# One-hot rows of the dense expert gates from bit products on TensorE

## The chip, the cores and the metric

The kernel runs on one core of a Trainium2 chip. The metric is device time in microseconds (us), from the first to the last instruction of one launch, as the median of several runs. The engines are named as in the profile: PE is TensorE (PEld its weight loads), DVE is VectorE, ACT is ScalarE, POOL is GpSimd, SP is SyncE, which issues most DMAs.

## The reference, cut to what matters

The program is a two-layer backbone over 512 latent and 256 context tokens of width 1024: a mixer and a PEER expert layer in each layer. The change lies in the expert layer alone:

```
def block(xt):                                       # 128 tokens
    s = scores of the token against 2 x 128 keys, for 8 heads
    sv, si = lax.top_k(s, 16)                        # per head and key set
    cand = sv[:, :, 0, :, None] + sv[:, :, 1, None, :]
    cs, ci = lax.top_k(cand, 16)                     # 16 experts (i, j) a head
    gate = softmax(cs)
    a = einsum('nd,nhkd->nhk', xt, u[eidx])
    w = gate * gelu(a)
    return einsum('nhk,nhkd->nd', w, v[eidx])
```

A token selects 8 x 16 = 128 experts out of 128 x 128, each named by two indices i and j below 128.

## The kernel before, in words

For 384 of the latent tokens (ND, three blocks of 128) the expert layer is computed densely: all 16384 experts, with a gate that is zero where an expert was not selected. The other tokens take their experts by gathered rows (`gather`, DMAs issued by POOL, sums on DVE).

`peer` (L1330 on) runs once a layer, in two stages. The routing stage has the pools `ps` (PSUM: tag `pj` with 2 buffers of one bank, `big` with 2 of two banks, `po` with 2 of one bank) and `wts`. `route` makes the scores (`scores`, top 16 by `top16` on DVE) and then, block by block and half by half, `select`, which leaves the indices fi, fj and the gate g as [128 tokens, 128 selections]. Its scratch comes from `alloc`, 5 buffers of [128, 1024] shared with the lists of the top 16. Once both halves of a dense block are selected, `gate_build` (L1044) makes its dense gates. In the same stage `dense_u` (L1105) computes the first product for 18 experts columns (layer 0) or 27 (layer 1) ahead, from weights that SP loads (L182) and that ACT and DVE or POOL split in two (L185, L188). The dense stage follows: 128 steps of first and second products (L1112, L1161), which multiply by the gates read back from DRAM (`load_gates`, L1139, L1151).

`gate_build` transposes fi, fj and g with TensorE (L1055), so that selections lie on the partitions and tokens in the free dimension, and splits each index in its upper and lower bits (L1056 to L1059). Then it goes through eight chunks of 16 tokens. For a chunk DVE compares the bits with a ramp (L1070, `up` and `low`, four instructions), POOL multiplies the low rows of j by the gate (L1073), and eight products of an upper and a lower row (L1084, `ghot`, [128, 4 tokens, 128]) give the one-hot rows of i and of j for four tokens each. DVE makes five of the eight, POOL three (`GENG`). For every token a matmul of the two rows (L1090, `gps`, 128x128, fp32) sums the 128 selections into the token's gates [i, j]. Eight tokens fill a `big` tile, which ACT copies to `G` [i, j, 16 tokens] (L1092), written with a step of 16 elements. One DMA a chunk, issued by ACT, puts G into DRAM (L1093). A layer has 24 chunks, 96 groups of four tokens ("pairs" of one-hot rows), 768 gate matmuls and 48 copies.

The order on each engine is set by the Tile scheduler, by program order as priority and by when it reckons an instruction to be ready; engines then run their queues in order. `issue_after` and `later` hold parts back. All waits are its own.

Of the kernel before, what the change touches and what calls it, by code (L numbers as in the profile page):

```python
# [22 lines left out]
ND = 384        # latent tokens whose experts are computed densely  # L23
# candidate segments of the 16x16 sums: rows a0..a1 keep their first nb columns
SEGS = [(0, 1, 16), (1, 2, 8), (2, 4, 5), (4, 8, 3), (8, 16, 1)]
NCAND = sum((b - a) * n for a, b, n in SEGS)
GENG = "vpvpvvvp"           # engines that make the one-hot rows in turn: Vector, Pool
UPRE = 18, 27               # by layer: experts (., j) whose first product runs ahead of the second
EARLY = 350                 # gathered rows of layer 0 that go ahead of its dense part
LATE = 64                   # of layer 0's, those that are left to the mixer of layer 1  # L30
# [30 lines left out]
def _cst_layout():  # L61
    off = 0
    for name, n in (("ident", 128), ("ones", 128), ("perm", 128), ("mf", 128), ("mb", 128),
                    ("iota", 128), ("start", 16), ("cos", 512), ("sin", 512)):
        CST[name] = (off, n)
        off += n
    return off
# [5 lines left out]
def constants():  # L73
# [27 lines left out]
    put("start", np.array(starts)[None, :])  # L101
    return c


class Kern:
    def __init__(self, ctx, tc, a, dbg=None):
# [8 lines left out]
        self.wcnt, self.wlo, self.ghot = 0, WL1, 0  # L115
# [12 lines left out]
        self.yd = self.dr.tile([2, D, 768], F32, name="yd")  # L128

# [10 lines left out]
    @contextmanager  # L140
    def mixing(self):
        """pools of the parts between the expert layers"""
        tc = self.tc
        with tc.tile_pool(name="wts", bufs=2, reuse_waits="tile") as self.pw, \
                tc.tile_pool(name="ps", bufs=1, space=bass.MemoryType.PSUM, reuse_waits="tile") as self.ps:
            yield
# [9 lines left out]
    def later(self, offset=1 << 20):  # L156
        """what is issued inside gives way to what is issued up to `offset` later"""
# [20 lines left out]
    def weight(self, src, shape):  # L178
        """src: DRAM AP of `shape` ([128, k, n], 1024 elements a row); returns (hi, lo)."""
# [28 lines left out]
    def projN(self, ps, w2, x, b):  # L208
        """ps [128 tok of block b, 256] = x^T w, w2 = the two halves of k."""
# [10 lines left out]
    def mod_prep(self):  # L220
# [9 lines left out]
        # column 1 adds up the partitions  # L230
# [4 lines left out]
    def mod(self, l, parts):  # L235
        """rows m_parts of layer l (streams ctx, lat) to DRAM; parts 1 and 4 as (1 + m) g."""
# [79 lines left out]
    def mod_rows(self, l, parts):  # L316
        """mod for the latents alone with the products on Vector, a step for 128 rows of the weights."""
# [18 lines left out]
    def mod_out(self, l, m, q, ps):  # L336
        """a quarter of part m from its product: bias, gain, to DRAM."""
# [20 lines left out]
    def rstd(self, ss, n, shape, scale=None):  # L358
        """(ss / n + eps) ** -0.5"""
# [16 lines left out]
    def xpose(self, x, xt, b):  # L376
        """x [128 tok, 1024] into xt = (hi, lo) [128, 8, T] at block b."""
# [11 lines left out]
    def norm1(self, l, s, src, nb, rows=None):  # L389
        """modulated norm of the blocks src[b]; returns their transposed halves."""  # L390
# [20 lines left out]
    def even_prep(self):  # L411
# [21 lines left out]
        # mLSTM gate rows: forward heads on partitions 0-3, backward heads on 32-35  # L433
# [10 lines left out]
    def gates(self, s, xt, nb, bb):  # L444
        """gate rows, stabilisers and the columns drawn from them, for blocks bb..bb+nb."""
# [33 lines left out]
        # columns  # L479
# [13 lines left out]
        # chunk totals on every partition  # L493
# [3 lines left out]
        # off-diagonal column biases QG[:, target, direction, source, head]  # L497
# [18 lines left out]
    def sigmoid(self, x, out, n):  # L516
        """out = exp(min(x, 0) - ln(1 + exp(-|x|))), n columns"""
# [8 lines left out]
    def ml_pair(self, s, xt, nb, bb, pr, P):  # L526
        """mLSTM heads 2 pr, 2 pr + 1 of blocks bb..bb+nb: projections; returns the rest,
        which writes the outputs transposed to DRAM."""
# [4 lines left out]
        # conv + silu of q (two padded copies) and k  # L533
# [22 lines left out]
        # v with a column of ones, output gate  # L556
# [28 lines left out]
        def front(hh, b):  # L585
# [21 lines left out]
            plan = []   # (direction, first slot, first source, count) off the diagonal  # L607
# [56 lines left out]
    def pipe(self, units, front, back):  # L664
        """front of a unit is issued ahead of the back of the one before it"""
# [856 lines left out]
```

## Time and profile before

| | |
|---|---|
| time of the runs, median of 3 | 4348.12 us (4344.39 to 4353.43) |
| span of the profiled execution | 4350.6 us |
| busy: PE, PEld | 3739.3, 3297.7 us |
| busy: DVE, ACT, POOL | 3715.8, 1603.3, 2683.4 us |
| DMA | 1093 MB, mean 251 GB/s |
| gate matmuls, L1090 | 1536, 231.8 us |
| one-hot products, L1084 | 240 on DVE, 144 on POOL |
| copies of the gates, L1092 | 96, 184.0 us |

Busy time is the time in which an engine had an instruction in work, and PE and PEld overlap. A mean over the whole span hides that the stages have different limits, so the stages are read one by one. The two gate stages are the short stretches from 1304 to 1514 us (layer 0) and from 3172 to 3385 us (layer 1). A line of the timeline merges neighbours of one kind, so that its length can hold short idle times; what stands in square brackets is the idle time ahead of it and what ended that.

### The profile page before, as it was taken

How to read it: one execution, taken by the hardware profiler on the slowest of the kernel's cores; microseconds unless marked ns; L12 is line 12 of the kernel's file. 1: busy time of each engine (PE TensorE's matmuls, PEld its weight loads, DVE VectorE, ACT ScalarE, POOL GpSimd, SP SyncE). 2: the span in 40 equal slices, each digit the busy share in tenths (PEclk: the TensorE clock that was granted, in tenths of full speed). 3: DMA queues.
4: the chain of work that ended last, by engine and by line, in shares of the span. 5: the costliest groups of instructions: out<-in, count | busy, mean ns of one | idle time of the engine just before them, and what ended most of it. 6: DMA issues, size and time to landing. Idle time of an engine off the chain costs nothing.

```text
span 4350.6 us, 58785 instructions
## 1 busy us (share of the span) xinstructions
PE 3739.3 (86%) x20576; PEld 3297.7 (76%) x20576; DVE 3715.8 (85%) x6089; ACT 1603.3 (37%) x2676; POOL 2683.4 (62%) x1886
## 2 busy tenths in 40 slices
PE   7977666756687699999999968899886999999999
PEld 5776654445567689988889857787875899999987
DVE  6479989979999998898989989747999887777788
ACT  4433433412115533333333325443245433333333
POOL 3146777656656677777878667112577676666664
PEclk9998888878798999999999989999989999999999
DMA  5554888788742499999899988423234987887878
GB/s 192 187 185 158 276 284 280 263 308 317 241 135 109 184 337 336 332 320 327 318 331 335 341 301 290 160 84 125 94 126 168 321 309 272 285 287 269 288 264 313
DMA packets 382487, 1093.10 MB, mean 251 GB/s; under 512 B 32671, under 2 KB 134375, under 8 KB 376046
## 3 DMA queue, kind: packets, MB, share of 16 engines
q0 software_dynamic: 147456, 536.94, 34.8%
q1 hardware_dynamic: 224942, 491.58, 32.9%
q10 hardware_dynamic: 9792, 60.82, 3.4%
q8 instruction: 162, 2.65, 0.2%
q14 instruction: 135, 1.11, 0.1%
HBM read 1020.96 MB, written 68.26 MB: 250 GB/s over the span
## 4 chain that ended last, share of the span: by engine, by line
PE 40%; DVE 25%; issue 15%; DMA 11%; POOL 7%; ACT 2%; SPq 0%; POOLq 0%; DVEq 0%; ACTq 0%
PE dacc L1161 17%; PE dA L1112 14%; POOL uv L998 4%; DVE ghot L1084 4%; DMA uv<-in_pr_u_dram,ix 3%; DMA draw<-in_uT_dram 3%; DVE junkv L1011 3%; DMA uv<-in_pr_v_dram,ix 2%; PE ops L214 1%; DVE wlo L188 1%; DVE pacc L1024 1%; PE pqps L204 1%; DVE sel L916 1%; DVE gup L1070 1%; DVE sel L913 1%
## 5 line engine op out<-in xcount | busy, mean ns | idle before, releaser
L1161 PE MATMUL dacc<-dhi,dw 128*128 128x512 f32 x3072 | 989.1, 392 | 3.4 <-ACT dw L1154 1.8
L998 POOL DMA_INDIRECT uv<-in_pr_v_dram,ix x512 | 685.6, 1339 | 405.0 <-DVE pacc L1024 297.6
L998 POOL DMA_INDIRECT uv<-in_pr_u_dram,ix x512 | 685.2, 1338 | 373.6 <-DVE pa L1011 204.3
L1011 DVE CUSTOM_DVE_ANT_0 junkv<-uv,x 128x1024 bf16<-128x1024 f32 x512 | 734.7, 1435 | 39.5 <-DMA uv<-in_pr_u_dram,ix 35.5
L1024 DVE SCALAR_TENSOR_TENSOR pacc<-uv,pw,pacc 128x1024 f32<-128x1024 f32 x508 | 705.1, 1388 | 26.9 <-DMA uv<-in_pr_v_dram,ix 23.0
L1161 PEld LDWEIGHTS dacc<-dhi,dw 128*128 128x128 f32 x3072 | 579.9, 189 | 120.7 <-ACT dw L1154 2.1
L1101 ACT CAST dhi<-draw 128x1024 fp32r<-128x1024 f32 x467 | 489.2, 1050 | 463.6 <-DMA draw<-in_uT_dram 165.9
L1161 PE MATMUL dacc<-dlo,dw 128*128 128x512 f32 x1536 | 604.4, 394 | 11.1 <-DVE dlo L1102 11.0
L1102 POOL TENSOR_TENSOR dlo<-draw,dhi 128x1024 fp32r<-128x1024 f32 x210 | 545.5, 2598 | 95.6 <-ACT dhi L1101 91.9
L188 POOL TENSOR_TENSOR wlo<-wraw,whi 128x1024 fp32r<-128x1024 f32 x111 | 280.0, 2523 | 426.0 <-ACT whi L185 282.1
L1151 DVE TENSOR_TENSOR dz<-dz,dG 128x384 f32<-128x384 f32 x256 | 402.4, 1585 | 89.9 <-ACT dz L1121 88.5
L1154 ACT CAST dw<-dz 128x384 fp32r<-128x384 f32 x256 | 131.4, 513 | 690.8 <-PE dacc L1161 669.8
L1102 DVE TENSOR_TENSOR dlo<-draw,dhi 128x1024 fp32r<-128x1024 f32 x257 | 336.1, 1308 | 27.3 <-ACT dhi L1101 18.1
L185 ACT CAST whi<-wraw 128x1024 fp32r<-128x1024 f32 x195 | 204.3, 1049 | 416.6 <-PE pqps L204 101.5
L1112 PE MATMUL dA<-xth,dhi 128*128 128x384 f32 x1688 | 334.8, 340 | 10.1 <-ACT dhi L1101 6.9
L1161 PEld LDWEIGHTS dacc<-dlo,dw 128*128 128x128 f32 x1536 | 289.8, 189 | 70.1 <-DVE dlo L1102 13.3
L1112 PE MATMUL dA<-xtl,dhi 128*128 128x384 f32 x1688 | 327.4, 335 | 0.0
L1112 PEld LDWEIGHTS dA<-xth,dhi 128*128 128x128 f32 x1688 | 305.1, 189 | 28.5 <-ACT dhi L1101 7.8
L1112 PE MATMUL dA<-xth,dlo 128*128 128x384 f32 x1688 | 326.7, 334 | 0.0
L1090 PE MATMUL gps<-ghot 128*128 128x128 f32 x1536 | 231.8, 307 | 104.5 <-DVE ghot L1084 80.2
L1090 PEld LDWEIGHTS gps<-ghot 128*128 128x128 f32 x1536 | 211.2, 216 | 126.3 <-issue 84.4
L1112 PEld LDWEIGHTS dA<-xtl,dhi 128*128 128x128 f32 x1688 | 296.7, 188 | 0.0
(379 smaller groups left out, 6836.6 us busy)
## 6 DMA issues: line engine op xcount, KB each, us to landing
draw<-in_pr_v_dram SPq DMA_DIRECT2D x256, 512.0 KB
draw<-in_uT_dram SPq DMA_DIRECT2D x211, 512.0 KB
wraw<-in_wb_dram SPq DMA_DIRECT2D x150, 512.0 KB
gd<-gch ACTq DMA_DIRECT2D x48, 1024.0 KB
dG<-gd SPq DMA_DIRECT2D x30, 1536.0 KB
wraw<-in_mod_t_dram SPq DMA_DIRECT2D x48, 512.0 KB
wraw<-in_uT_dram SPq DMA_DIRECT2D x45, 512.0 KB
wraw<-in_mod_w_dram SPq DMA_DIRECT2D x32, 512.0 KB
```

What stands on the lines that cost most here:

```text
L185: nc.scalar.copy(hi, raw)
L188: eng.tensor_tensor(lo, raw, hi.bitcast(F32), op=OP.subtract)
L998: nc.gpsimd.indirect_dma_start(out=t, out_offset=None, in_=a[table], in_offset=bass.IndirectOffsetOnAxis(ap=ix[:, c:c + 1], axis=0))
L1011: nc.vector.tensor_tensor_reduce(out=junk, in0=u, in1=x, op0=OP.mult, op1=OP.add, scale=1.0, scalar=0.0, accum_out=A[:, c:c + 1])
L1024: nc.vector.scalar_tensor_tensor(acc, v, W[:, c:c + 1], acc, op0=OP.mult, op1=OP.add)
L1084: eng.tensor_tensor(h.rearrange("p t (a b) -> p t a b", b=16), up[:, e, t0:t0 + 4, :].unsqueeze(3).broadcast_to([128, 4, 8, 16]), low[:, e ...
L1090: nc.tensor.matmul(ps[:, t0 - 8 * q + t, :], hot[0][:, t, :], hot[1][:, t, :], start=True, stop=True)
L1101: nc.scalar.copy(hi, raw)
L1102: eng.tensor_tensor(lo, raw, hi.bitcast(F32), op=OP.subtract)
L1112: nc.tensor.matmul(A, u[ui][:, k, :], xt[xi][:, k, 0:ND], start=(i == 0), stop=(i == 23))
L1151: nc.vector.tensor_tensor(z3, z3, self.G[:, :, j % JG, :], op=OP.mult)
L1161: self.nc.tensor.matmul(acc[b][:, h, :], w[wi][:, 128 * b:128 * b + 128], v[vi][:, 512 * h:512 * h + 512], start=(j == 0 and i == 0), stop ...
```

## The change

The one-hot rows are no longer products of an upper and a lower row on DVE and POOL. Each index is split in seven bits, on DVE, in the layout that it has (tokens on the partitions). Bit e is kept as 2^e or 0, beside a plane of ones, as bf16. The planes of a block are written to DRAM (`bd`, 512 KB) and read back four chunks at a time (256 KB) with (token, bit) on the partitions. There a matmul with constant coefficients (`gB`, block diagonal over the 16 tokens of a chunk) gives, for a token and each value n, 1 minus the number of bits that differ from those of n: 1 where the index is n, 0 or less elsewhere. One matmul of 512 columns makes four tokens. ACT takes the positive part of those of i (Relu), DVE that of j times the gate (`scalar_tensor_tensor`). The gate matmuls stay. The copy of the products walks with indices outside and 8 tokens inside, so that its writes are runs of 8 elements and its reads of PSUM step by 128 elements.

New constants are `coef` (128 columns) and `tmask` (16 columns) in `cst`. `gate_build` gets `alloc` and takes three of the shared buffers a block. `fi` and `fj` become halves of one tile. Comments and docstrings are gone.

```
-GENG = "vpvpvvvp"           # engines that make the one-hot rows in turn: Vector, Pool
...
+    bits = (p[None, :] >> np.arange(7)[:, None]) & 1
+    coef = np.concatenate([(2.0 * bits - 1.0) / 2.0 ** np.arange(7)[:, None], 1.0 - bits.sum(0)[None, :]], 0)
+    put("coef", np.tile(coef, (16, 1)))
+    put("tmask", p[:, None] // 8 == np.arange(16)[None, :])
...
+        self.bd = self.dr.tile([ND // 128, 1024, 256], BF16, name="bd")
...
+    def gate_consts(self):
+        nc = self.nc
+        self.gB = self.wk.tile([128, 16, 128], BF16, name="gB")
+        nc.vector.tensor_tensor(self.gB, self.c("coef")[:, None, :].broadcast_to([128, 16, 128]),
+                                self.c("tmask").unsqueeze(2).broadcast_to([128, 16, 128]), op=OP.mult)
+
+    def gate_build(self, b, sel, alloc):
         nc, wk = self.nc, self.wk
...
+        _, g, fij, _ = sel
+        pl = alloc().bitcast(BF16).rearrange("p (e x) -> p e x", e=8)
+        nc.gpsimd.memset(pl[:, 7, :], 1.0)
+        for s in range(2):
+            bu = alloc().bitcast(U32).rearrange("p (e x) -> p e x", e=8)
+            nc.vector.tensor_copy(bu[:, 7, :], fij[:, 128 * s:128 * s + 128])
+            for e in range(7):
+                nc.vector.tensor_scalar(bu[:, e, :], bu[:, 7, :], 1 << e, None, op0=OP.bitwise_and)
+            nc.vector.tensor_copy(pl[:, 0:7, 128 * s:128 * s + 128], bu[:, 0:7, :])
+        nc.sync.dma_start(self.bd[b].rearrange("(t e) x -> t e x", e=8), pl)
+        pt = self.po([128, 128], "gtp")
+        nc.tensor.transpose(pt, g, self.ident)
+        gT = wk.tile([128, 128], F32, name="gT", tag="gT", bufs=2)
+        nc.scalar.copy(gT, pt)
         for c in range(8):
...
+            if c % 4 == 0:
+                bits = wk.tile([128, 4, 256], BF16, name="gbits", tag="gbits", bufs=2)
+                nc.sync.dma_start(bits, self.bd[b].rearrange("(c p) x -> p c x", p=128)[:, c:c + 4, :])
             G = wk.tile([128, 128, 16], F32, name="gch", tag="gch", bufs=2)
             for q in range(2):
                 ps = self.big([128, 8, 128], "gps")
                 for t0 in (8 * q, 8 * q + 4):
                     hot = []
+                    for s in range(2):
+                        d = self.po([128, 4, 128], "gds")
+                        nc.tensor.matmul(d, bits[:, c % 4, 128 * s:128 * s + 128], self.gB[:, t0:t0 + 4, :],
+                                         start=True, stop=True)
                         h = wk.tile([128, 4, 128], F32, name="ghot", tag="ghot", bufs=6)
...
+                        if s == 0:
+                            nc.scalar.activation(h, d, AF.Relu)
+                        else:
+                            t = 16 * c + t0
+                            nc.vector.scalar_tensor_tensor(
+                                h, d, 0.0, gT[:, t:t + 4].unsqueeze(2).broadcast_to([128, 4, 128]),
+                                op0=OP.max, op1=OP.mult)
                         hot.append(h)
                     for t in range(4):
                         nc.tensor.matmul(ps[:, t0 - 8 * q + t, :], hot[0][:, t, :], hot[1][:, t, :],
                                          start=True, stop=True)
-                nc.scalar.copy(G[:, :, 8 * q:8 * q + 8].rearrange("p j t -> p t j"), ps)
+                nc.scalar.copy(G[:, :, 8 * q:8 * q + 8], ps.rearrange("p t j -> p j t"))
             nc.scalar.dma_start(self.gd[8 * b + c], G)
```

## Rows read from the trace of the kernel before

**Rows 1.** Stretches: length; busy PE, PEld, DVE, ACT, POOL; granted clock, DMA share, GB/s.
```profile
1304.00:1514.00 210.00, 151.03 (x964) 140.31 (x962) 198.46 (x293) 111.09 (x86) 141.48 (x109) 0.90 0.37 143
...
3450.00:4200.00 750.00, 750.00 (x3792) 682.76 (x3791) 591.53 (x579) 274.11 (x364) 504.90 (x284) 1.00 0.82 285
...
3172.00:3385.00 213.00, 157.48 (x988) 145.51 (x987) 201.98 (x304) 115.61 (x97) 148.34 (x116) 0.91 0.40 153
```
**Rows 2.** Chain that ended last, 1290 to 1530 us, by line; two pieces in layer 1.
```profile
by line: DVE ghot L1084 32.0%; issue 18.0%; DVE gup L1070 10.6%; DVE glow L1070 8.0%; POOL glow L1073 3.4%; DVE wlo L188 3.2%; DMA draw<-in_uT_dram 3.1%; DVE sel L965 2.7%; POOL ghot L1084 2.5%; DVE sel L969 2.3%; POOL dlo L1102 2.2%; DVE s
...
3384.67 3.88 DMA gd<-gch
3388.62 3.98 DMA dG<-gd
```
**Rows 3.** Timeline of one chunk: start, length, instructions, idle before.
```profile
1492.53 0.62 DVE L1070 TENSOR_TENSOR gup<-cst,gcol 128x128 f32<-128x128 f32 x2
1493.07 0.74 DVE L1070 TENSOR_TENSOR glow<-cst,gcol 128x256 f32<-128x256 f32 x2
1493.74 6.13 DVE L1084 TENSOR_TENSOR ghot<-gup,glow 128x512 f32<-128x512 f32 x5
...
1498.52 1.13 PE L1090 MATMUL gps<-ghot 128*128 128x128 f32 x8 [0.34 <-DVE ghot L1084]
1499.69 1.91 ACT L1092 COPY gch<-gps 128x1024 f32<-128x1024 f32 x1 [1.89 <-PE gps L1090]
1499.79 0.63 DVE L1070 TENSOR_TENSOR gup<-cst,gcol 128x128 f32<-128x128 f32 x2
```
**Rows 4.** Instructions by line or tile: count, duration min/median/max (ns), first and last start.
```profile
L1084 DVE TENSOR_TENSOR ghot<-gup,glow x240: 665/694/6202, 1303.5 to 3379.8; 128x512 f32<-128x512 f32 x120
...
L1070 DVE TENSOR_TENSOR glow<-cst,gcol x96: 403/411/2553, 1291.0 to 3371.4; 128x256 f32<-128x256 f32 x96
L1070 DVE TENSOR_TENSOR gup<-cst,gcol x96: 346/356/2480, 1295.4 to 3370.0; 128x128 f32<-128x128 f32 x96
```
**Rows 5.** The same, of the lines whose operations are nearest to the new ones.
```profile
L523 DVE SCALAR_TENSOR_TENSOR sg<-og,sg x6: 677/684/1489, 84.8 to 488.3; 128x512 f32<-128x512 f32 x6
...
L976 DVE TENSOR_SCALAR sel<-sel x20: 165/181/2261, 329.1 to 3232.3; 128x64 uint32<-128x64 uint32 x20
...
L1057 DVE TENSOR_SCALAR gcu<-gcu x6: 271/278/2460, 1287.2 to 3257.3; 128x256 uint32<-128x256 uint32 x6
...
L1161 PE MATMUL dacc<-dhi,dw x3072: 386/389/632, 1525.1 to 4339.8; 128*128 128x512 f32 x192
...
L383 ACT CAST xth<-xps x26: 1002/1012/1033, 46.8 to 2966.2; 128x1024 fp32r<-128x1024 f32 x26
...
L1092 ACT COPY gch<-gps x96: 1865/1912/2002, 1307.7 to 3382.7; 128x1024 f32<-128x1024 f32 x96
```
**Rows 6.** Groups by line: shapes, count, busy us, mean ns, idle before and its releasers.
```profile
L869 ACT COPY pq<-pqps 128x512 f32<-128x512 f32 x32 | 18.7, 586 | 115.3 <-PE pss L872 90.7 <-PE pqps L204 24.6
```
**Rows 7.** Chain, dense stage: start, length, and what, merged.
```profile
3416.14 4.12 PE dacc L1161 x18
3420.26 4.18 PE dA L1112 x24
```
**Rows 8.** Weight loads of the gate matmuls at both levels, SP's issues, a block's first step.
```profile
1285.83 0.41 DVE L1056 CAST gcu<-gtp 128x256 uint32<-128x256 f32 x1
...
1301.13 40.07 SPq L182 DMA_DIRECT2D wraw<-in_uT_dram  x6
...
1304.29 2.05 PE L1090 MATMUL gps<-ghot 128*128 128x128 f32 x8
...
1498.49 0.97 PEld L1090 LDWEIGHTS gps<-ghot 128*128 128x128 f32 x8 [0.50 <-issue]
```
**Rows 9.** Tile dA in the gate stages: length; busy PE, PEld, ACT; clock, DMA.
```profile
1304.00:1514.00 210.00, 40.81 (x193) 34.99 (x191) 4.40 (x9) 0.90 0.37 143
3172.00:3385.00 213.00, 46.70 (x217) 41.73 (x216) 4.95 (x10) 0.91 0.40 153
```

More of the change, by code (lines that the diff above doesn't have):

```diff
@@ L63, in _cst_layout @@
     for name, n in (("ident", 128), ("ones", 128), ("perm", 128), ("mf", 128), ("mb", 128),
-                    ("iota", 128), ("start", 16), ("cos", 512), ("sin", 512)):
+                    ("iota", 128), ("start", 16), ("cos", 512), ("sin", 512),
+                    ("coef", 128), ("tmask", 16)):
         CST[name] = (off, n)
@@ L114, in __init__ @@
         self.wk = None
-        self.wcnt, self.wlo, self.ghot = 0, WL1, 0
+        self.wcnt, self.wlo = 0, WL1
         nc = self.nc
@@ L889, in route @@
             out.append([sq(pg, "ix", 3, U32), sq(pg, "gt", 3), None, None] if b >= nd else
-                       [None] + [sq(wk, n, 3) for n in ("dgt", "fi", "fj")])
+                       [None, sq(wk, "dgt", 3), wk.tile([128, 256], F32, name="fij", tag="fij", bufs=3), None])
         pick = lambda b, half: self.select(l, V[b], I[b], out[b], half, alloc)
@@ L901, in route @@
                     if half == 1:
-                        after(b, out[b])
+                        after(b, out[b], alloc)
             for b in range(nd, nb):
@@ L933, in select @@
         V, I = V[:, hs, :], I[:, hs, :]
-        ix, g, fi, fj = (t if t is None else
-                         t[:, 64 * half:64 * half + 64].rearrange("p (h k) -> p h k", h=4) for t in out)
-        if fi is None:
-            fi, fj = W(4, 16), W(4, 16)
+        part = lambda t, o=0: t[:, o + 64 * half:o + 64 * half + 64].rearrange("p (h k) -> p h k", h=4)
+        ix, g, fij, _ = out
+        g, ix = part(g), ix if ix is None else part(ix)
+        fi, fj = (W(4, 16), W(4, 16)) if fij is None else (part(fij), part(fij, 128))
         IF = W(8, 16)
@@ L1042, in resid @@
         return h
-    def gate_build(self, b, sel):
-        nc, wk = self.nc, self.wk
-        iota = self.c("iota")
-        _, g, fi, fj = sel
-        cols = wk.tile([128, 5, 128], F32, name="gcol", tag="gcol", bufs=1)
-        cu = wk.tile([128, 2, 128], U32, name="gcu", tag="gcu", bufs=1)
-        pt = self.po([128, 3, 128], "gtp")
-        for n, src in enumerate((fi, fj, g)):
-            nc.tensor.transpose(pt[:, n, :], src, self.ident)
-        nc.vector.tensor_copy(cu, pt[:, 0:2, :])
-        nc.vector.tensor_scalar(cu, cu, 15, None, op0=OP.bitwise_and)
-        nc.vector.tensor_copy(cols[:, 2:4, :], cu)
-        nc.vector.tensor_tensor(cols[:, 0:2, :], pt[:, 0:2, :], cols[:, 2:4, :], op=OP.subtract)
-        nc.scalar.copy(cols[:, 4, :], pt[:, 2, :])
-        TG = 16
-        for c in range(8):
-            if 16 * c % TG == 0:
-                tk = slice(16 * c, 16 * c + TG)
-                up = wk.tile([128, 2, TG, 8], F32, name="gup", tag="gup", bufs=2)
-                low = wk.tile([128, 2, TG, 16], F32, name="glow", tag="glow", bufs=2)
-                for n, (t, at) in enumerate(((up, iota[:, 0:128:16]), (low, iota[:, 0:16]))):
-                    m = t.shape[-1]
-                    for e in range(2):
-                        nc.vector.tensor_tensor(
-                            t[:, e], at[:, None, :].broadcast_to([128, TG, m]),
-                            cols[:, 2 * n + e, tk].unsqueeze(2).broadcast_to([128, TG, m]), op=OP.is_equal)
-                nc.gpsimd.tensor_tensor(low[:, 1], low[:, 1],
-                                        cols[:, 4, tk].unsqueeze(2).broadcast_to([128, TG, 16]), op=OP.mult)
@@ L1079, in gate_build @@
                     hot = []
-                    for e in range(2):
+                    for s in range(2):
+                        d = self.po([128, 4, 128], "gds")
+                        nc.tensor.matmul(d, bits[:, c % 4, 128 * s:128 * s + 128], self.gB[:, t0:t0 + 4, :],
+                                         start=True, stop=True)
                         h = wk.tile([128, 4, 128], F32, name="ghot", tag="ghot", bufs=6)
-                        eng = nc.gpsimd if GENG[self.ghot % len(GENG)] == "p" else nc.vector
-                        self.ghot += 1
-                        eng.tensor_tensor(
-                            h.rearrange("p t (a b) -> p t a b", b=16),
-                            up[:, e, t0:t0 + 4, :].unsqueeze(3).broadcast_to([128, 4, 8, 16]),
-                            low[:, e, t0:t0 + 4, :].unsqueeze(2).broadcast_to([128, 4, 8, 16]), op=OP.mult)
+                        if s == 0:
[5 more added lines that the diff above has]
+                                op0=OP.max, op1=OP.mult)
                         hot.append(h)
@@ L1337, in peer @@
                 alloc = lambda: pool.tile([128, D], F32, name="sel", tag=tag, bufs=5)
+                self.gate_consts()
                 sel = self.route(l, xt, nb, nd, alloc, self.gate_build)
```

## The prediction

> **What bounds the kernel now.** I read the stages first, one by one. In the dense stage PE is busy all the time (750 of 750 us) at the full granted clock [rows 1]: what ends a routing stage earlier moves that block of work forward as it is, so time saved ahead of it is time saved in all. Nothing of the change lies in the dense stage, so the two gate stages decide. There DVE is busy 198.5 of 210 us and 202 of 213, PE 151 and 157, ACT 111 and 116, POOL 141 and 148, at clocks of 0.90 and 0.91 [rows 1]. The chain of waits says the same: one-hot products and comparisons on DVE hold over half of it (32.0 + 10.6 + 8.0%), most of the rest being issue time and POOL's part [rows 2]. One chunk on the timeline shows why: from one set of comparisons to the next it is 1499.79 - 1492.53 = 7.26 us, and five products on DVE take 6.13 of it [rows 3], 1.2 us each, where one alone takes 0.665 [rows 4]; they are stretched while POOL makes its three. PE waits for them (0.34 us ahead of its eight), ACT for PE (1.89 us) [rows 3]. 24 chunks x 7.26 = 174 us; the remaining 24 us of DVE's 198.5 are selections and splits of weights.
>
> **What goes.** Those 174 us of DVE, and all of POOL's products. Nothing else on DVE runs as slowly as before, since POOL has little left to do there.
>
> **What comes on DVE.** 96 `scalar_tensor_tensor` a layer from PSUM, 128x512: the same operation took 0.684 [rows 5], 96 x 0.684 = 66 us. The bits: a mask on 64 columns takes 0.18 and on 256 columns 0.28 [rows 5], so 0.21 on 128. For an index that is 7 x 0.21, a conversion of 0.2 and one of 896 elements, which by the slope of those two rows takes 0.6 and at one element a nanosecond 1.0; 2.3 to 2.7 us, 4.6 to 5.4 a block, 15 a layer. DVE then has 66 + 15 + 24 = 105 us to do: no longer the bound.
>
> **What comes on PE.** 192 matmuls of 512 columns a layer. Dense ones follow each other by 4.12 / 18 = 0.229 us [rows 7], 44 us. The 768 gate matmuls take 0.97 / 8 = 0.121 each when nothing holds them [rows 8], 93 us, and 193 and 217 first products in these stretches [rows 9] 4.18 / 24 = 0.174 [rows 7], 34 and 38 us. PE's own work is thus 171 and 175 us, against stages of 210 and 213. That is the floor.
>
> **What comes on ACT.** 96 Relus of 128x512 at the 0.586 of such a copy [rows 6], 56 us; 111 - 48 x 1.912 = 19 us are other work [rows 1, 5]. The price of the 48 turned copies is shown nowhere. Contiguous on both sides, 1024 elements take 1.012; with writes stepping by 16 elements they take 1.912 now [rows 5]. The new one writes runs and reads with a step. A stepped read is the upper comparison of DVE: its ramp is read with a step of 16, and 128 elements take 0.356, where 256 without a step take 0.411 and 512 take 0.665 [rows 4]. That line gives 0.27 for 128, so the step costs some 0.6 ns an element, and 1024 of them 0.6 us. I take 1.6 us, by this row, and keep 1.0 to 1.9, and more than 1.9 as a rival. ACT's sum is 19 + 56 + 77 = 152 (124 to 167).
> [...]
>
> **What bounds after.** All three sums lie under the stages, so the chain through a pair of one-hot rows has to be looked at. `po` has two buffers, one for each row of a pair. When DVE has read one, program order puts the four gate matmuls of that pair ahead of the next product into the freed buffer. A round is: DVE 0.684, hand-over 0.04 (copy at 1499.69, matmuls done at 1499.65 [rows 3]), four gate matmuls 4 x 0.121 = 0.485, the product 0.39 to its end [rows 5], hand-over 0.04: 1.64 us. ACT has 0.586 and half a copy (0.8) in the same round, 1.39. At the clock of now (0.90 [rows 1]) PE's 0.875 become 10% longer: 1.73, and 96 rounds are 166 us. To this I add, as estimates: DVE's other work (39 us, 0.22 of the time, pieces of about 1 us, half of one met on average) 96 x 0.22 x 0.5 = 10; first products between, each up to 0.174, 3; ACT's other work ahead of a Relu, 5. 184 us in layer 0, 185 in layer 1.
>
> **Lead-in.** From the first step on a block's indices (1285.83) to the first gate matmul (1304.29) it is 18.5 us now [rows 8]. After: bits 5, DRAM there and back 3.88 + 3.98 (a larger pair of such transfers [rows 2]), first round 1.2, some 14 us: 4.5 less. But both transfers go through SP, behind weight loads that wait for their buffers; SP needed 40.07 us for six [rows 8], 6.7 each, and two such waits would be 9 more than now. I take +4. Of the later blocks the bits are made during the chunks before them (eight rounds of 7 us), which hides them; without that cover they cost 14 us a block. The three scratch buffers of a block are held until its transfer has landed, 4 us a block, and delay selections on a DVE that has room: nothing, at most 8 a layer. `gB` is one DVE instruction of 2048 elements, 4 x 0.6 = 2.4 us by [rows 4], on DVE ahead of the top 16s: 0 to 2.4, taken 1. POOL's memset and the narrower transposes: nothing. After the last copy the same write, read-back and first step follow as now.
>
> **Sum.** Layer 0: 184 + 4 + 1 - 210 = -21. Layer 1: 185 + 4 + 1 - 213 = -23. Together -44 on a span of 4350.6. The median of the runs is 2.5 us under that span: 4348.1 - 44 = 4304.
>
> **Rivals.**
> 1. PE's floor. If the scheduler lets the next product go ahead of the gate matmuls, the round opens and PE alone is the limit: 171 + 5 - 210 = -34 and 175 + 5 - 213 = -33, 4281. For it: such an order needs only that the freed buffer is seen before the second row is ready. Against: ACT would need 1.39 of 1.8 us a round without a gap, and the clock to be full.
> 2. The copy stays at 1.9 (the change doesn't do what its second half says). Two pairs on ACT are then 2 x 0.586 + 1.92 + one turn of a buffer (0.04 + 0.39 + 0.04) = 3.56, 48 times 171, and 19 us of other work fill part of the turns: about 195 with the lead-in. -15 and -12, 4321. For it: the step is 128 elements, not 16. Against: the row of the stepped read.
> 3. The clock falls: slower. [...] For it: once the first products are used up, PE has 0.95 of 1.73 us to do, 55%. Against: over the stage it is 55% and 18% of first products, as much as the 72% that now are granted 0.90 [rows 1].
> 4. The stepped read costs over 1.9. At three cycles in place of one (1.012 + 2 x 0.85 = 2.7) two pairs on ACT are 4.35, 209 us and 19 more: +20 a layer, 4390. It turns against the change from about 2.3 us.
> 5. Waits of the fixed order eat it all (loads behind the transfers, the planner's prices off): 4348.
>
> **Chances.** Forecast 0.46; floor 0.14; slow copy 0.14; clock 0.1; costlier copy 0.06; nothing 0.1. The forecast's own bounds are 4290 to 4322 (lead-in -4 to +9, the estimates of 18 us at half or one and a half, twice). The range takes in the floor and its lead-in at the better end (4268) and leaves out the upper half of the clock's case and the costlier copy: 4268 to 4374. A measurement of this kernel tells about 0.2% (8.7 us) from no change. Faster by more: forecast, floor and most of the slow copy, 0.72; same 0.13; slower 0.15.
>
> **What would show it.** DVE's busy share of the gate stage falls from 0.94 to about 0.6, POOL's to under 0.3. The new products are spaced by rounds of about 1.7 us, with PE waiting for DVE's row. The copy's mean is the direct reading of its step: 1.0, 1.6 or 1.9. The Relu takes 0.59, DVE's row 0.68, the clock stays near 0.9. The gate stages shrink to 185 to 192 us from first gate matmul to last copy, and the dense stage keeps its 750 us pace. The prediction is wrong if SP's transfers leave a gap of over 10 us ahead of a block, if the clock drops under 0.8, or if stages without any gates change their length by more than these do, because the scheduler has put their work in another order.

## The result and the profile after

The changed kernel takes 4405.7 us (median of 4 runs, 4394.8 to 4414.6), the kernel before 4346.3 in the same comparison (4340.9 to 4353.4): 1.0131 times as long, 95% interval 1.0106 to 1.0155. That is 59 us slower; 4304 was predicted, with 4268 to 4374 as the range. The profiled execution has a span of 4393.0 us; it is the fastest of its four, so the trace accounts for 42 of the 59 us.

The page after, the chain of work that ended last by line, and three groups by line (shapes and count, then busy us and mean ns of one, idle time before them and what ended it). The one-hot products and comparisons on DVE have left the page, and the new products' waiting has taken their place:

```profile
PE dacc L1171 14%; PE dA L1122 13%; POOL uv L1005 6%; PE gps L1100 5%; DMA draw<-in_uT_dram 3%; DMA uv<-in_pr_v_dram,ix 3%; DVE ghot L1095 3%; DMA uv<-in_pr_u_dram,ix 2%; DVE junkv L1018 2%; PE ops L221 1%; POOL dlo L1112 1%; DVE wlo L195 1%; PE pqps L211 1%; DVE pacc L1031 1%; DVE sel L923 1%
...
L1100 PEld LDWEIGHTS gps<-ghot 128*128 128x128 f32 x1536 | 189.6, 194 | 201.5 <-DVE ghot L1095 198.7
...
L1095 DVE SCALAR_TENSOR_TENSOR ghot<-gds,gT 128x512 f32<-128x512 f32 x192 | 132.5, 690 | 246.1 <-PE gds L1088 246.1
...
L1100 PE MATMUL gps<-ghot 128*128 128x128 f32 x1536 | 224.9, 290 | 111.0 <-DVE ghot L1095 110.6
```

DVE's rows (L1095) are busy for 132.5 us and wait 246.1 for the product (L1088); PE's gate matmuls (L1100) wait 110.6 for DVE's row. Each waits for the other.

Stretches of the kernel after (start:end, length, busy us and instructions of PE, PEld, DVE, ACT, POOL, granted clock, DMA share, GB/s): the gate stages of both layers, from the first gate matmul to the end of the last copy, and 50 us of each with gates alone.

```profile
1290.00:1543.00 253.00, 194.08 (x1184) 146.44 (x1184) 126.31 (x302) 122.18 (x184) 34.89 (x37) 0.98 0.34 131
3171.00:3427.00 256.00, 196.39 (x1188) 148.43 (x1186) 128.66 (x300) 126.46 (x193) 44.25 (x42) 0.97 0.35 136
1400.00:1450.00 50.00, 36.88 (x232) 25.19 (x232) 16.06 (x24) 24.82 (x37) 0.00 (x0) 1.00 0.32 129
3250.00:3300.00 50.00, 37.09 (x236) 25.39 (x236) 15.91 (x23) 24.36 (x36) 0.00 (x0) 1.00 0.40 163
```

Beside [rows 1], DVE's share has fallen from 0.94 to 0.50 and POOL's from 0.67 to 0.14, and the clock has risen from 0.90 to 0.98. The stages have grown all the same, from 210 and 213 us to 253 and 256. In the pure stretches PE is busy for 37 of 50 us, ACT for 25, DVE for 16: no engine is full. That is what a chain looks like. Its rounds on the timeline (start, length, instruction, count, idle time before it and what ended that):

```profile
3301.60 1.16 PE L1100 MATMUL gps<-ghot 128*128 128x128 f32 x8 [0.57 <-DVE ghot L1095]
...
3302.59 0.59 PE L1088 MATMUL gds<-gB,gbits 128*128 128x512 bf16 x2
3303.01 0.69 DVE L1095 SCALAR_TENSOR_TENSOR ghot<-gds,gT 128x512 f32<-128x512 f32 x1 [1.47 <-PE gds L1088]
...
3303.75 1.16 PE L1100 MATMUL gps<-ghot 128*128 128x128 f32 x8 [0.57 <-DVE ghot L1095]
...
3304.95 1.01 ACT L1102 COPY gch<-gps 128x1024 f32<-128x1024 f32 x1 [1.13 <-PE gps L1100]
3305.17 0.69 DVE L1095 SCALAR_TENSOR_TENSOR ghot<-gds,gT 128x512 f32<-128x512 f32 x1 [1.47 <-PE gds L1088]
```

From DVE row to DVE row it is 3305.17 - 3303.01 = 2.16 us: the row 0.69, eight gate instructions and only then the product that DVE waits for. The copy takes 1.01.

Where the 42.4 us between the two profiled spans (4350.6 and 4393.0) arise: layer 0's gate stage ends at 1542.9 instead of 1513.6 (+29.3); its dense stage is 19 us shorter from first to last `dacc` matmul (984.1 against 1003.1; 8.5 of these are waits of PE, 13.2 before and 4.7 after, which the change doesn't touch), and layer 1's first gate matmul starts at 3170.6 instead of 3172.2, so that another 13 us come back between the last `dacc` matmul and there. Layer 1's stage is 44 us longer again and ends 42.3 later, and that stays until the end. The `dacc` matmuls of layer 0, before and after (count, duration min/median/max in ns, first and last start):

```profile
L1161 PE MATMUL dacc<-dhi,dw x1536: 386/389/632, 1525.1 to 2528.2; 128*128 128x512 f32 x192
...
L1171 PE MATMUL dacc<-dhi,dw x1536: 387/389/398, 1555.6 to 2539.7; 128*128 128x512 f32 x192
```

### The profile page after: what moved, and what is told of

Same layout as the page of the kernel before. It is cut to its first block, busy times and chain, and to the rows that moved or that the text cites. A ratio compares the mean times of both kernels' runs of the same rounds, so it can differ in the third digit from the quotient of the medians.

```text
span 4393.0 us, 59129 instructions
## 1 busy us (share of the span) xinstructions
PE 3801.6 (87%) x20948; PEld 3289.8 (75%) x20948; DVE 3530.0 (80%) x5935; ACT 1625.0 (37%) x2868; POOL 2444.4 (56%) x1700
## 4 chain that ended last, share of the span: by engine, by line
PE 41%; DVE 22%; issue 15%; DMA 11%; POOL 8%; ACT 2%; SPq 0%; POOLq 0%; DVEq 0%; ACTq 0%
PE dacc L1171 14%; PE dA L1122 13%; POOL uv L1005 6%; PE gps L1100 5%; DMA draw<-in_uT_dram 3%; DMA uv<-in_pr_v_dram,ix 3%; DVE ghot L1095 3%; DMA uv<-in_pr_u_dram,ix 2%; DVE junkv L1018 2%; PE ops L221 1%; POOL dlo L1112 1%; DVE wlo L195 1%; PE pqps L211 1%; DVE pacc L1031 1%; DVE sel L923 1%
## 5 line engine op out<-in xcount | busy, mean ns | idle before, releaser
L1100 PEld LDWEIGHTS gps<-ghot 128*128 128x128 f32 x1536 | 189.6, 194 | 201.5 <-DVE ghot L1095 198.7
L1095 DVE SCALAR_TENSOR_TENSOR ghot<-gds,gT 128x512 f32<-128x512 f32 x192 | 132.5, 690 | 246.1 <-PE gds L1088 246.1
L1100 PE MATMUL gps<-ghot 128*128 128x128 f32 x1536 | 224.9, 290 | 111.0 <-DVE ghot L1095 110.6
```

The lines of the kernel that those rows point to most:

```text
L1095: nc.vector.scalar_tensor_tensor(h, d, 0.0, gT[:, t:t + 4].unsqueeze(2).broadcast_to([128, 4, 128]), op0=OP.max, op1=OP.mult)
L1100: nc.tensor.matmul(ps[:, t0 - 8 * q + t, :], hot[0][:, t, :], hot[1][:, t, :], start=True, stop=True)
```

## The experiments

The theory (A): the round is a chain through the two `po` buffers, as the prediction said, but with eight gate instructions in it, not four. The rivals: ACT's part or the copy sets the round (B); PE's own work is the limit, or the loss lies elsewhere (C). Times stand beside the kernel before, which took 4347 to 4352 us in the three comparisons.

### Four product buffers

```
-                        d = self.po([128, 4, 128], "gds")
+                        d = (self.pj if s else self.po)([128, 4, 128], "gds")
```

> The changed kernel with one edit: the product of the j rows takes its PSUM tile from the two buffers of `pj`, so that a pair of one-hot rows has four buffers in all. Theory A, the stage is set by a chain through the two `po` buffers: a round of four tokens is DVE's row 0.69 + eight gate matmul instructions 8 x 0.121 = 0.97 + the product 0.39 + two hand-overs 0.08 = 2.13 us (2.16 measured), and each waits for the other. With four buffers the products no longer wait for the row just read: the round falls to PE's own work, 0.97 + 2 x 0.22 = 1.4 us, 96 x 1.4 = 135 us and some 35 of first products of the dense stage: gate stages of 175 to 190 us against 253 and 256, and the kernel at 4406 - 2 x 70 = 4265 (4250 to 4320), faster than the kernel before. Rival B, the ACT part is the limit (two Relus 1.2 and a copy 1.0 in two rounds, 2.2 of 4.3 us, with waits of its own): no more than 10 us a layer. Rival C, PE's work is itself the limit, or the time was lost elsewhere by another order of the work: within 10 us of 4406.

4388.6 us, 1.0084 [1.0059, 1.0109] of the kernel before: 17 us better than the change (the two intervals just touch), not 86 to 156. The round did what A says. From its timeline, two rounds:

```profile
1384.99 1.16 PE L1100 MATMUL gps<-ghot 128*128 128x128 f32 x8
...
1386.42 1.05 PE L1100 MATMUL gps<-ghot 128*128 128x128 f32 x8
...
1387.75 1.16 PE L1100 MATMUL gps<-ghot 128*128 128x128 f32 x8
```

2.76 us for two, 1.38 a round, with no idle time on PE. The gate stages shrink to 151 us (1277.0 to 1428.0) and 155. The gain went elsewhere: line 1355 takes the tiles of the dense stage's first products (`dA`) from `pj` too. The rows' products took that ring, and the first products came after the gates. This experiment's group of layer 0's 432 of them (count, duration min/median/max in ns, first and last start), one of three:

```profile
L1122 PE MATMUL dA<-xth,whi x144: 333/334/687, 1463.1 to 1537.8; 128*128 128x384 f32 x144
```

In the changed kernel the same group runs from 1251.5 to 1349.9, inside the selections. Here PE has 3.6 us to do in 3100 to 3150 and the first `dacc` starts at 1553.0, as late as in the change (1555.6). So the chain through two buffers is confirmed by the round, and the time shows what a buffer costs that another part needed.

### The product first

```
+            nxt = rows(*groups[n + 1])      # products, ReLU and row of the next four tokens
             for t in range(4):
                 nc.tensor.matmul(ps[...], hot[0][:, t, :], hot[1][:, t, :], ...)
```

> The changed kernel with another program order and the same two `po` buffers: the products, ReLU and row of the next four tokens stand ahead of the gate matmuls of these four. Theory A, the chain is long because the next product stands behind eight gate matmul instructions (0.97 us) although its buffer is free: with the product ahead, DVE's next row is made while PE does the gate matmuls. The round is then the larger of DVE's 0.69 + 0.39 + 0.08 = 1.16 and PE's 0.97 + 2 x 0.22 = 1.41: gate stages of 175 to 190 us, the kernel at 4265 (4250 to 4330). If the scheduler sets the same order all the same, the round stays 2.16 and the time 4406 (within 10). Rival C (PE's sum is the limit, or the loss lies elsewhere): within 10 us of 4406.

4282.9 us, 0.9837 [0.9812, 0.9863]: 123 us better than the change, and 1.6% faster than the kernel before. Timeline of it, PE and DVE:

```profile
3261.35 0.69 PE L1084 MATMUL gds<-gB,gbits 128*128 128x512 bf16 x2
...
3261.88 1.05 PE L1107 MATMUL gps<-ghot 128*128 128x128 f32 x8
3262.08 0.69 DVE L1091 SCALAR_TENSOR_TENSOR ghot<-gds,gT 128x512 f32<-128x512 f32 x1 [0.78 <-PE gds L1084]
...
3262.77 0.59 PE L1084 MATMUL gds<-gB,gbits 128*128 128x512 bf16 x2
...
3263.20 1.05 PE L1107 MATMUL gps<-ghot 128*128 128x128 f32 x8
3263.47 0.69 DVE L1091 SCALAR_TENSOR_TENSOR ghot<-gds,gT 128x512 f32<-128x512 f32 x1 [0.70 <-PE gds L1084]
```

DVE's row now lies beside the gate matmuls of the group before, where it used to stand between them; rounds of 1.39 and 1.48, two in 2.87, and PE is busy for 48.9 of 50 us. Same buffers, same instructions, same copy: the order of the program alone, and with it PE's queue, was worth 123 us. B and C fall as bounds of the changed kernel.

### Gate matmuls of one instruction

```
-                        h = wk.tile([128, 4, 128], F32, name="ghot", tag="ghot", bufs=6)
+                        h = wk.tile([128, 4, 128], F32R, name="ghot", tag="ghot", bufs=6)
```

> The changed kernel with the one-hot rows held as F32R in place of F32, so that each gate matmul is one instruction in place of two; the gates are rounded to that type on the way, all else is computed as before. This gives the round the four instructions that the prediction counted. Theory A (the round is a chain, and the prediction missed four of its eight gate matmul instructions): the round is 0.69 + 4 x 0.121 + 0.39 + 0.08 = 1.65 us, 1.65 to 1.8 measured; 96 x 0.5 = 48 us a layer come back: gate stages near 205 us, the kernel at 4406 - 96 = 4310 (4295 to 4335), close to the predicted 4304. If a one-pass matmul of 128 columns takes as long as the two passes of now (0.24 us), the round stays 2.13. Rival B (ACT): the round stays above 2.0. Rival C (the loss lies elsewhere): within 15 us of 4406.

4422.2 us, 1.0163 [1.0139, 1.0187]: 16 us worse than the change (the intervals of the two ratios overlap), although PE issues 384 gate instructions fewer a layer. A miss. Its stretches (columns as above):

```profile
1300.00:1350.00 50.00, 45.99 (x254) 43.41 (x254) 49.12 (x182) 21.55 (x35) 25.00 (x33) 0.93 0.32 116
1350.00:1400.00 50.00, 36.41 (x113) 20.16 (x114) 25.35 (x41) 26.12 (x44) 7.04 (x3) 0.53 0.23 93
1400.00:1450.00 50.00, 42.45 (x130) 23.23 (x129) 14.52 (x21) 22.32 (x33) 0.00 (x0) 0.50 0.33 133
```

The granted clock fell from 1.00 to 0.50 for the rest of the stage in both layers. On the timeline where it fell (0.75 on the mean from 1350 to 1355, 0.50 from there), PE waited twice for DVE's row, 2.68 and 2.49 us, with 0.96 us of work between 1350 and 1355. At that clock four gate instructions take 0.92 (1422.59 to 1423.51), and the round 2.35 us. What the prediction's third rival said of the changed kernel, that the clock falls, came true in a variant that does less. What the count of instructions costs at the full clock this run couldn't tell.

### The old copy

```
-                nc.scalar.copy(G[:, :, 8 * q:8 * q + 8], ps.rearrange("p t j -> p j t"))
+                nc.scalar.copy(G[:, :, 8 * q:8 * q + 8].rearrange("p j t -> p t j"), ps)
```

> The changed kernel with the copy of the gate products turned back: PSUM is read in runs and the SBUF tile is written with a step of 16 elements, as in the kernel before, 1.91 us a copy in place of 1.01. Theory A (chain of DVE and PE): ACT then has 2 x 0.6 + 1.91 = 3.1 of the 4.3 us of two rounds and room left; a Relu that waits behind a copy can come up to 0.9 us late, but in the chain it is the DVE row that is waited for: within 15 us of 4406, up to 30 if the Relu takes the chain's place in one round of two (48 x 0.3 us a layer). Rival B (ACT's part sets the round): 48 x 0.9 = 43 us a layer, 4490. The second half of the change is then worth only what this run shows.

4406.2 us, as the change (4405.7), with copies of 1.90 in place of 1.01. ACT is busy for 68.3 of 100 us (1400 to 1500). In the changed kernel the second half of the change is worth nothing.

### The old copy with the product first

The edit before, in the kernel with the product first.

> The kernel with the product first (e2_product_first, rounds of 1.43 us, 4283) with the copy of the gate products turned back to 1.90 us in place of 1.01. In the changed kernel itself that made no difference (4406.2 against 4405.7), since two rounds of 2.16 left ACT room. Here two rounds are 2.87 us and ACT's part of them two ReLUs and a copy, 2 x 0.60 + 1.90 = 3.1. If the copy's direction counts as soon as the chain is open: rounds of 1.55 to 1.6, 48 x 0.25 to 0.35 = 12 to 17 us a layer, 4283 + 24 to 34 = 4307 to 4317. If ACT has slack in other places that takes it up, or PE's rows wait in buffers: within 8 us of 4283. If the copy is worth its full 0.89 us: 4283 + 85 = 4368.

4350.5 us, 0.9991 [0.9979, 1.0004] of the kernel before: 68 us more than with the new copy, over twice what I expected from ACT's own sum (two ReLUs and a copy, 3.1 us). Its timeline:

```profile
1421.39 1.90 ACT L1110 COPY gch<-gps 128x1024 f32<-128x1024 f32 x1 [0.78 <-PE gps L1107]
...
1423.10 1.10 ACT L1088 ACTIVATE ghot<-gds 128x512 f32<-128x512 f32 x2
...
1423.77 0.38 PE L1084 MATMUL gds<-gB,gbits 128*128 128x512 bf16 x1 [0.75 <-ACT ghot L1088]
...
1425.07 1.89 ACT L1110 COPY gch<-gps 128x1024 f32<-128x1024 f32 x1 [0.87 <-PE gps L1107]
```

Two rounds take 1425.07 - 1421.39 = 3.68 us. Two ReLUs wait behind the copy; PE's product waits 0.75 us for a ReLU; the next copy waits 0.87 for the gate matmuls. ACT is in the chain now. The same 0.89 us of a copy is worth nothing under one order and 68 of 96 x 0.89 = 85 us under the other.

### The new copy in the kernel before

```
-                nc.scalar.copy(G[:, :, 8 * q:8 * q + 8].rearrange("p j t -> p t j"), ps)
+                nc.scalar.copy(G[:, :, 8 * q:8 * q + 8], ps.rearrange("p t j -> p j t"))
```

> The kernel before with the copy alone turned as in the change (PSUM read with a step of 128 elements, SBUF written in runs of 8), 1.01 us a copy in place of 1.91. There DVE is busy for 198 of 210 us and ACT for 111, and ACT waits for PE (1.89 us a chunk): the copy is not on the path. Expected within 9 us of the kernel before (4351). Rival, the copy holds the buffers that PE's gate matmuls write: 48 x up to 0.9 us a layer, up to 86 us faster.

4349.9 us, 0.9994 [0.9984, 1.0004], with copies of 1012 ns in place of 1912: nothing, as expected of a kernel bound by DVE.

### One-instruction gate matmuls, issued twice

`for t in (0, 0, 1, 1, 2, 2, 3, 3)` in the kernel with the F32R rows.

> e3_one_pass with each gate matmul issued twice into the same place, so that PE has eight instructions a round again (the second writes the same numbers). If the low clock of e3_one_pass came from PE's having too little to do in a round: clock back at 0.95 or over, rounds of 2.16 as in the changed kernel, 4406 (within 12). If it came from the type of the matmul: clock 0.50, a round of 0.69 + 8 x 0.23 + 0.63 + 0.08 = 3.2 us, 4422 + 2 x 96 x 0.85 = 4585.

4576.4 us. Clock 0.50 again, rounds of 3.20 us (DVE rows at 1431.00, 1434.20, 1437.41), PE busy for 88.5 of 100 us. My explanation, too little work on PE, gave 4406 and fell; by number the other one, the type of the matmul, was right (4585). The stretch (columns as above):

```profile
1380.00:1480.00 100.00, 88.52 (x313) 60.66 (x312) 21.76 (x32) 33.84 (x49) 0.00 (x0) 0.50 0.20 80
```

### One-instruction gate matmuls with the product first

The F32R edit in the kernel with the product first.

> The kernel with the product first (e2_product_first) and the one-hot rows as F32R (as in e3_one_pass, which rounds the gates to that type). In e3_one_pass PE had 0.92 us to do in a round and waited for DVE in the rest; its granted clock was 0.50 in all pure gate stretches, and the round went to 2.4 us. Theory: what lowered the clock is that PE idled for more of the round, not the type of the matmul. With the product first, the round at the full clock is set by DVE, 0.69 + 0.39 + 0.08 = 1.16 us, or by ACT, 0.60 + 0.51 = 1.11; PE is busy for about 0.9 of it, more than in the changed kernel (1.4 of 2.16, clock 0.97 to 1.00): the clock stays over 0.9, rounds 1.2, gate stages near 165 us, 4283 - 2 x 25 = 4233 (4220 to 4260). Rival: matmuls of this type hold the clock down whatever the share: clock 0.50, a round of 4 x 0.23 + 2 x 0.43 = 1.8 us bound by PE, 4283 + 2 x 96 x 0.37 = 4354.

4256.6 us, 0.9781 [0.9763, 0.98]. Clock 1.00 with PE busy for 55 of 70 us (1380 to 1450), two rounds in 2.60 us. So the type alone doesn't hold the clock down either. It is the fastest of all, but its one-hot rows, with the gates in them, are written as F32R.

```profile
1380.00:1450.00 70.00, 55.20 (x320) 40.47 (x319) 36.25 (x53) 56.32 (x82) 0.00 (x0) 1.00 0.51 207
```

### Each gate matmul twice

`for t in (0, 0, 1, 1, 2, 2, 3, 3)` in the changed kernel.

> The changed kernel with each gate matmul issued twice into the same place (the second writes the same numbers), sixteen gate instructions a round in place of eight. If these instructions stand in the chain between DVE's row and the next product, as the trace says, all of the added 8 x 0.121 = 0.97 us lengthens the round: 2.16 + 0.97 = 3.13 us, 96 x 0.97 = 93 us a layer, 4406 + 186 = 4592 (4570 to 4610), at a granted clock of about 1. Rival: the round is set by something beside PE (ACT's part, DVE's waits) and hides a part of them: under 4500.

4567.3 us, 162 more than the change (expected 186; just under the span that I gave). On its timeline:

```profile
1422.59 2.05 PE L1100 MATMUL gps<-ghot 128*128 128x128 f32 x16 [0.57 <-DVE ghot L1095]
...
1424.89 0.69 DVE L1095 SCALAR_TENSOR_TENSOR ghot<-gds,gT 128x512 f32<-128x512 f32 x1 [2.36 <-PE gps L1100]
...
1425.64 2.05 PE L1100 MATMUL gps<-ghot 128*128 128x128 f32 x16 [0.57 <-DVE ghot L1095]
```

Rounds of 1425.64 - 1422.59 = 3.05 us at a clock of 1.00: eight instructions more lengthen the round by 0.89, 0.11 each. Nothing covers them; they stand in the chain one for one.

### The count of the prediction, with PE kept at work

```
 (with F32R rows)
+                    nc.tensor.matmul(ps[:, t0 - 8 * q:t0 - 8 * q + 4, :], bits[:, c % 4, 0:128],
+                                     self.gB[:, t0:t0 + 4, :], start=True, stop=True)
                     for t in range(4):
                         nc.tensor.matmul(ps[:, t0 - 8 * q + t, :], hot[0][:, t, :], hot[1][:, t, :], ...)
```

> e3_one_pass with one more matmul of 512 columns a round, bit products written into a place of `ps` that the gate matmuls write over afterwards, so that PE has something to do while DVE makes the row. In e3_one_pass the granted clock fell to 0.50 and the round of four gate instructions could not be read at full speed. If the clock holds here, the round is what the prediction counted, 0.69 + 4 x 0.11 + 0.39 + 0.08 = 1.6 us, 1.65 to 1.75 with what lies between: 4406 - 96 x 0.45 x 2 = 4320 (4300 to 4335). If it falls again: rounds of 2.4 to 2.6 and 4420 to 4455. If the missing four instructions are not what the prediction had wrong: full clock and rounds of 2.1.

4316.0 us, 0.9919 [0.9901, 0.9936]: 90 us better than the change. The clock is 1.00 with PE busy for 78 of 100 us (1380 to 1480); it had fallen to 0.74 and 0.58 in the two 5 us from 1350 on, and came back. Its timeline:

```profile
1421.01 0.66 PE L1102 MATMUL gps<-ghot 128*128 128x128 f32 x4 [0.57 <-DVE ghot L1095]
...
1421.94 0.69 DVE L1095 SCALAR_TENSOR_TENSOR ghot<-gds,gT 128x512 fp32r<-128x512 f32 x1 [0.99 <-PE gds L1088]
...
1422.69 0.66 PE L1102 MATMUL gps<-ghot 128*128 128x128 f32 x4
...
1423.62 0.69 DVE L1095 SCALAR_TENSOR_TENSOR ghot<-gds,gT 128x512 fp32r<-128x512 f32 x1 [0.98 <-PE gds L1088]
```

Four gate instructions, rounds of 1.68 us: the prediction's 1.64. Four in place of eight, at the full clock, moves the round from 2.16 to 1.68, and the kernel from slower to faster. The type of the rows and the added matmul changed along with the count; an instruction of the new type takes about as long as one of the old (four in 0.50 us), and the added matmuls lie beside DVE's row.

### The same with two such matmuls

```
+                    for s in range(2):
+                        nc.tensor.matmul(ps[:, t0 - 8 * q:t0 - 8 * q + 4, :], bits[:, c % 4, 128 * s:128 * s + 128],
+                                         self.gB[:, t0:t0 + 4, :], start=True, stop=True)
```

The expectation's "two more" are two a round in all, in place of one; its sum counts them so.

> As g2_one_pass_fill1 with two more matmuls of 512 columns a round. Where four of them come together ahead of a product, 4 x 0.22 + 0.22 = 1.1 us of PE's stand in a gap of 0.77: 0.3 more in one round of two, rounds of 1.8 on the mean at the full clock, 4406 - 96 x 0.36 x 2 = 4337 (4315 to 4350). If the clock falls here too, PE's 4 x 0.23 + 4 x 0.43 = 2.6 us are behind each other: rounds of 2.8 to 3, 4530 to 4570.

4320.5 us, 0.9933 [0.9915, 0.9952]: 4.5 us more than with one (the two intervals overlap), 17 less than the 4337 expected. Clock 1.00, rounds of 1.70 on the mean (1419.87, 1421.58, 1423.25, 1424.96). Nearly all of the added work lies beside DVE's row: here what PE does while the chain is at DVE is free; what it does in between costs its full length (each gate matmul twice).

## Why the prediction was wrong, step by step

**The step that failed: "four gate matmuls 4 x 0.121 = 0.485".** 0.121 is the time of one instruction, and a gate matmul of fp32 is two. What I counted as a layer's 768 gate matmuls are 768 instructions for 384 tokens, so four tokens are eight: 0.97. The rows said so: 768 by 24 chunks of 16 tokens is two a token, and [rows 3] shows them in groups of x8. The kernel before was described in the same way: its "768 gate matmuls" a layer are 384 matmuls. The sum of PE's work used the 768 and was right; the round used the tokens. With eight, the prediction's own line gives 0.684 + 0.04 + 0.97 + 0.39 + 0.04 = 2.12 (measured 2.16), the stage 96 x 2.12 + 18 = 222, and with the lead-in +17 and +15 in place of -21 and -23: about 4380, slower. That count alone had the sign. This leaves out the 10% that the prediction added to PE's part for a clock of 0.90; with them the round is 2.26 and the sum about 4405, which is what was measured, but by luck: the clock was 0.98, and the time lay in the next term. Four runs with different edits bear the round out: fewer instructions (1.68), more (3.05), the product moved ahead of them (1.43), other buffers (1.38).

**The second term that was mis-sized: 18 us of interference.** Of 253 us, 96 x 2.16 = 207 are rounds, 46 are not (49 in layer 1). The stage's first part shows them, DVE's rows alone in three stretches of the kernel after:

```profile
1290.00:1350.00 60.00, 6.11 (x10) 0.94 0.32 115
1350.00:1360.00 10.00, 1.24 (x2) 0.83 0.00 0
1360.00:1550.00 190.00, 58.25 (x85) 0.98 0.37 147
```

Ten rows in the first 60 us; the kernel before got through 136 / 8 = 17 groups in the 60 us from its first gate matmul. The prediction spread DVE's other work evenly over the rounds (0.22 of the time). It lies at the start instead, and there DVE is full: 57.9 of 60 us. The stretches below give DVE's busy time by tile. The first two are the changed kernel: selections with their index bits (`sel`), and splits of the first products' weights (`wlo`). The next two are the run with four buffers in its first 60 us: its rows, and its selections. The last is the kernel before: its selections.

```profile
1290.00:1350.00 60.00, 46.57 (x187) 0.94 0.32 115
1290.00:1350.00 60.00, 7.52 (x5) 0.94 0.32 115
...
1277.00:1337.00 60.00, 21.64 (x33) 0.99 0.39 156
1277.00:1337.00 60.00, 41.23 (x181) 0.99 0.39 156
...
1304.00:1364.00 60.00, 26.88 (x66) 0.89 0.28 106
```

This chain goes through two engines and queues twice in a round, behind a block of first products on PE (eight take 1.39 us on the timeline) and behind the selections on DVE. With four buffers, and the first products and their splits out of the way, DVE is as full (58.8 of 60 us) but makes 33 rows; the remainder of that stage is 151 - 96 x 1.38 = 19 us, about what I had estimated for all. With them it is 46 to 60 in every other variant at the full clock that I worked out (57 with the product first, 47 with four instructions). So 27 to 38 us go with the first products, their splits or the two buffers more; no run parts the three. The prediction's 3 us for the first products had only one of them in the way at a time.

**The start was better than forecast, mostly not by the lead-in.** The first gate matmul of layer 0 starts at 1290.1, 14 us before that of [rows 8], where I had allowed 5 more. From the first step on the block's indices it is 1290.1 - 1271.0 = 19.1 us, against 18.5 before and 22.5 forecast: 3.4 us better. The rest came from ahead of it: that first step came 14.8 us earlier (1271.0 against the 1285.83 of [rows 8]), since the block's last selection on DVE began at 1269.8 instead of 1281.9. The prediction's sum had no term for that.

```profile
L1068 DVE CAST sel<-fij x6: 211/224/1278, 1271.0 to 1325.6; 128x128 uint32<-128x128 f32 x6
...
L1100 PE MATMUL gps<-ghot x768: 270/275/582, 1290.1 to 1541.6; 128*128 128x128 f32 x192
```

Layer 0's end is the sum of the three: 50 us off the forecast (+29 for -21) is 41 by the round (96 x 0.43), 28 by the interference, -19 by the earlier start.

**The copy.** I took 1.6 between 1.0 and 1.9; it is 1.012, as a copy contiguous on both sides [rows 5]. Its reads of PSUM step by 512 bytes and its writes are runs of 32. My second rival, a copy that stays at 1.9, falls with it; the 1.6 came from a row of another engine ([rows 4], DVE). None of this moved the time, since ACT had room (old copy: 4406.2).

**What held.** DVE was the bound and is relieved (0.50 of the stage, though full in its first 60 us); the row takes 0.69, the Relu 0.60; two buffers and the product behind the gate matmuls set the round. The clock didn't fall in the changed kernel (0.98): third rival wrong here. The prediction's range leaves out the upper half of this case, by a price that no run of this kernel shows; where the clock did fall to 0.50, the round was 2.35 us with four gate instructions and the kernel took 4422.2, and 3.20 us and 4576.4 with the four issued twice. An estimate for the changed kernel's eight, from the 2.05 that they took [rows 8] (granted clock 0.50 from 1304.2 to 1306.4 us) and the longest product of 512 columns, 0.632 [rows 5], is 0.684 + 0.08 + 2.05 + 0.63 = 3.4. The first rival, "the next product goes ahead of the gate matmuls", is the version with the product first: 4281 by the prediction, 4282.9 measured. That is luck, since it agrees better than its parts do: the stages take 195 and 197 us, not 176 and 180; layer 0's ends 22 us earlier than in the kernel before, layer 1's starts 38 and ends 54 earlier.

**Smaller slips of the working, none of which decides.** In the second rival 195 - 213 is -18, not -12, which makes 4315 of its 4321. The forecast's own bounds (4290 to 4322) are about those of one term moved at a time; the lead-in and the 18 us together give 4270 to 4332. The floor with the better lead-in is 4265, not 4268.

**What stays open.** Why the clock stayed at 0.50 in two of the five variants with F32R rows (one instruction, and the same twice) and was 1.00 in the other three, where it had dipped at about the same place and come back (0.58 from 1355 to 1360 with one more matmul; over 1350 to 1400 0.90 on the mean with two, 0.83 with the product first). Neither PE's busy share (88.5% at 0.50, 78% at 1.00) nor the type of the matmul tells them apart. Nor was it followed up what besides 8.5 us of PE's waits shortened the dense stage of layer 0, nor what gave the 13 us ahead of layer 1's gates and the 14.8 ahead of layer 0's.

## What to carry to other kernels

When a chain crosses two engines, take the instructions of one round from the timeline, as counted there, and check them against the total by the number of rounds: a program's matmul and an instruction of the engine are not the same thing (here 384 fp32 gate matmuls a layer were 768 instructions). An engine that is half idle over a stage can be full in its first part (here DVE, busy for 0.50 of the stage and for 57.9 of its first 60 us), so the other work in a chain's way is read there and not spread over the stage. Where a freed buffer's next producer stands behind other work in its engine's queue, that work is in the chain (here eight gate instructions, in rounds of 2.16 us); put the producer ahead of it (1.43) before adding buffers (1.38, but 4388.6 us against 4282.9), and look who else takes buffers from the ring that is borrowed. What a cheaper step is worth (here the copy: 0 or 68 us) depends on whether it lies in the chain, so it is measured again after the chain has changed.

## What the runs showed of the hardware

- In the changed kernel ACT reads PSUM with a step of 512 bytes and writes SBUF in runs of 32 bytes in 1012 ns for 128x1024, as long as the contiguous copy of [rows 5] takes; in the kernel before, writes with a step of 64 bytes and contiguous reads took 1912.
- An fp32 matmul of 128x128 is two instructions of 0.11 to 0.12 us at a granted clock of 1.00 (768 a layer for 384 tokens; 0.97 us for the weight loads of eight [rows 8], 0.89 for the eight more of each gate matmul twice). With F32R rows it is one, 0.125 (1421.01 to 1421.51 for four, with one more matmul a round).
- With four gate instructions a round in place of eight (gate matmuls of one instruction) the granted clock went from 1.00 to 0.50 for the rest of the stage, around two waits of 2.68 and 2.49 us, and the kernel took 4422.2 us; with one matmul of 512 columns more a round, in time that was idle, the clock fell at the same place (0.74 and 0.58 in the 5 us from 1350 and from 1355), was 1.00 from 1360 on, and the kernel took 4316.0.
